# A GEMM by seven products in an fp32 trunk: two of its block sums grow in other buffers, one of them from on-chip memory, and are issued at other steps

## The chip, the cores and the metric

One NeuronCore of a Trainium2 chip runs the whole program. The metric is the device time of one execution in microseconds. "Before" was run three times: 1407.56, 1402.65 and 1401.54 us, median 1402.65.

## The reference

Two layers in float32 on x of 512 x 1024, each a token mixer and a dense MLP, pre-normed and modulated by a conditioning vector. Layer 0 mixes by chunked attention, layer 1 by spatial gating, which is where the change works:

```python
def chunked_spatial_gating(h, w_in, v_gain, w_s, b_s, w_out):
    B, S, _ = h.shape
    nw = S // SG_WINDOW
    z = jax.nn.gelu(h @ w_in, approximate=False)          # 512x1024 @ 1024x6144
    u, v = jnp.split(z, 2, axis=-1)
    v = rms_norm(v, v_gain).reshape(B, nw, SG_WINDOW, SG_GROUPS, SG_HALF // SG_GROUPS)
    ...
    vm = jnp.einsum('gij,bnjgc->bnigc', w, v) + b_s.T.astype(v.dtype)[None, None, :, :, None]
    return (u * vm.reshape(B, S, SG_HALF)) @ w_out
...
def reference(...):
    ...
        x = x + g1 * y
        h = rms_norm(x, norm_ffn[i]) * (1.0 + sc2) + sh2
        x = x + g2 * squared_relu_mlp(h, ffn_w1[i], ffn_w2[i])
```

## The kernel before

**Arithmetic.** Every large product is done in three matmuls (`mm3`, its matmuls are line 92): `Split` makes of a float32 tile its high part, by a cast on ACT (line 485, 128x1024), and the rest, by a subtract on DVE (line 486), and high x high, high x low and low x high are summed.

**Seven products.** `seven` (line 613) multiplies by a 1024x1024 piece of a weight in 2x2 blocks of 512x512, with seven products where the plain way has eight. Each block comes in two halves `s_` = 0, 1 of 512 KB. The names of the right blocks in the code are x = B00, z = B10, w = B01, y = B11. The steps run in the order m = 0, 1, 2, 4, 3, 5, 6; m = 0, 1 and 4 multiply by a block itself (x, z, y), the others by a sum: m = 2 by x after x += w, m = 3 by that x after x += y, m = 5 by B01 + B11, m = 6 by B10 plus the x of m = 3. `own` says which of the four sums DVE makes (`plus`, line 630, from a loaded block). The others are made by a DMA that adds to what is there: `grow`, line 627, issued by GpSimd (POOL), reads 512 KB from DRAM and adds it into a block's buffer.

**Who calls it.** The gate's halves of `b_w_in` (`Gate(p)`, p = 1, 2) had own = (2, 3, 5, 6), all on DVE. `Mix(p)`, p = 0, 1, 2, the other half, had own = (2, 3): its m = 5 and m = 6 sums grow by DMA, twelve DMAs in all (3 passes x 2 sums x 2 halves). The FFN's second product had own = (). A step has four parts, `load`, `right` (sums and Splits), `left` and `mult`, and `Run(steps, 4, 3)` calls a step's load 4 and 3 ticks, and its right and left 3 ticks, ahead of its mult.

**Buffers.** A tile takes one of 49 slots of 4 KB per partition (`Slots`), handed out in the order in which they were freed. So whoever first writes a new tile waits for the last users of the tile that had the slot before; which tile that is follows from the order of all frees.

**Mixing.** When a tile of the gate half is ready, `v_store` (line 1423) stores it to the DRAM tensor `vd` (512 KB, issued by ACT). `row_scales` (line 1547 on) makes the rows' scales from the sums of squares, once the gate is done. `Mix.put` gathers a product's outputs, applies Gelu (line 1585), and `Mix.mix` then scales v (line 1593), splits it (cast on ACT, line 1597, and subtract on DVE, line 1598), mixes the positions by matmuls, multiplies (line 1611), transposes on PE (line 1618) and copies out (line 1622). The program goes gate p = 1, 2, then Mix p = 0, a down projection, Mix p = 1, Mix p = 2, and the second down projection.

**Order of the work.** The engines' orders are made by a scheduler from the program as it is written; in a tile name as `s3_856_7615` the first number is the slot and the second counts the tiles. `tc.issue_after` holds an instruction back, in that order, behind another one.

Of the kernel before, what the change touches and what calls it, by code (L numbers as in the profile page):

```python
# [13 lines left out]
ALU = mybir.AluOpType  # L14
AX = mybir.AxisListType

P = 128
# [8 lines left out]
SGH = 3072  # L26
# [26 lines left out]
def trunk_kernel(  # L53
# [20 lines left out]
    V, A, G, T, SP = nc.vector, nc.scalar, nc.gpsimd, nc.tensor, nc.sync  # L74
# [13 lines left out]
    def bank():  # L88
        return PS.get([P, 512], F32)
# [4 lines left out]
    def mm3(ps, lh, ll, rh, rl, start, stop, more=False):  # L94

        mm(ps, lh, rh, start, False, more)
        mm(ps, lh, rl, False, False, more)
        mm(ps, ll, rh, False, stop, more)
# [278 lines left out]
    loaded = [None]  # L377
# [232 lines left out]

    waited = [None]

    def seven(left, src, y, own=()):


        raw, op, ps = {}, {}, {}

        def block(i, j, s_):
            r0 = i * 512 + s_ * 256
            return src[r0:r0 + 256, j * 512:j * 512 + 512].rearrange("(k p) n -> p k n", p=P)  # L620

        def load(name, i, j, s_):
            raw[name, s_] = t, n = SL.get([P, 2, 512], F32)
            SP.dma_start(t, block(i, j, s_))

        def grow(i, j, name, s_):
            G.dma_start(raw[name, s_][0], block(i, j, s_), accum_op=ALU.add)  # L627

        def plus(a, b, s_):
            V.tensor_tensor(raw[a, s_][0], raw[a, s_][0], raw[b, s_][0], ALU.add)  # L630

        def drop(name, s_):
            SL.free(raw.pop((name, s_))[1])

        def right(m, name, add, s_):

            if m == 2 and 2 in own:
                plus("x", "w", s_)
                if 5 not in own:
                    drop("w", s_)  # L640
            if m == 5 and 5 in own:
                name = "w"
                plus("w", "y", s_)
                drop("y", s_)
            if m == 6 and 6 in own:
                plus("x", "z", s_)
                drop("z", s_)
            loaded = m in (3, 5, 6) and m not in own
            with tc.issue_after(waited[0].ins) if loaded and waited[0] is not None else nullcontext():
                op[m, s_] = Split(raw[name, s_][0], [P, 2, 512])  # L650
            if m == 4 and 3 in own:
                plus("x", "y", s_)
            if add is None:
                if not (m == 1 and 6 in own):
                    drop(name, s_)
            elif {0: 2, 2: 3, 4: 5, 3: 6}[m] not in own:
                grow(*add, name, s_)

        def mult(m, acc, first, outs, done, s_):
            a, b = left.op[m], op.pop((m, s_))  # L660
            for u in range(2):
                if first and s_ == 0:
                    ps[acc, u] = bank()
                p, pi = ps[acc, u]
                c = slice(u * P, u * P + P)
                for k in range(2):
                    kk = 2 * s_ + k
                    ah, al, bh, bl = a.hi[:, kk, c], a.lo[:, kk, c], b.hi[:, k, :], b.lo[:, k, :]
                    mm3(p, ah, al, bh, bl, first and kk == 0, kk == 3, not first)
                if s_:  # L670
                    for i, j, o, whole in outs:
                        y.put(2 * i + u, j, p, o, whole)
                    if done:
                        PS.free(pi)
            b.free()
            if s_:
                left.done(m)

        def prep(m, s_):
            if s_ == 0:  # L680
                left.prep(m)

        add, sub = ALU.add, ALU.subtract
        plan = (
            (0, ("x", 0, 0), ("x", (0, 1)), ("z", True, ((0, 0, add, False),), False)),
            (1, ("z", 1, 0), ("z", None), ("y", True, ((0, 0, add, False),), True)),
            (2, None, ("x", (1, 1)), ("v", True, ((1, 1, add, False),), False)),
            (4, ("y", 1, 1), ("y", (0, 1)), ("v", False, ((0, 1, add, False),), True)),
            (3, None, ("x", (1, 0)), ("z", False, ((0, 1, sub, False),), False)),
            (5, None, ("y", None), ("z", False, ((1, 1, sub, False),), False)),  # L690
            (6, None, ("x", None), ("z", False, ((1, 0, add, True),), True)),
        )

        def loads(m, b, s_):
            if m == 2 and 2 in own:
                load("w", 0, 1, s_)
            if b:
                load(*b, s_)

        return [  # L700
            Step(
                lambda m=m, b=b, s_=s_: loads(m, b, s_),
                lambda m=m, r=r, s_=s_: right(m, *r, s_),
                lambda m=m, s_=s_: prep(m, s_),
                lambda m=m, p=p, s_=s_: mult(m, *p, s_),
            )
            for m, b, r, p in plan for s_ in range(2)
        ]
# [38 lines left out]
    def ffn(l, norm, rows, cols, after, bgn, lag=1):  # L747
# [53 lines left out]
        def down_steps(q):  # L801
            steps = seven(Spent(lambda: quarters(q)), ffn_w2[l][q * 1024:(q + 1) * 1024, :], y)

            def mult_last(f=steps[-1].mult):
                f()
                bg(bgn.pop(0) if bgn else 0)

            steps[-1].mult = mult_last
            return steps
# [606 lines left out]
    kept = Kept(lambda: norm.blocks)  # L1416
# [57 lines left out]
    def gate_steps(cb):  # L1474

        raw, op, ps = {}, {}, {}

        def load(n):
            t, i = raw[n] = SL.get([P, 2, 512], F32)
            c0 = SGH + cb * 512  # L1480
            SP.dma_start(t, b_w_in[0][n * 256:n * 256 + 256, c0:c0 + 512].rearrange("(k p) n -> p k n", p=P))

        def right(n):
            t, i = raw.pop(n)
            op[n] = Split(t, [P, 2, 512])
            SL.free(i)

        def mult(n):
            w = op.pop(n)
            for t in range(NT):  # L1490
                if n == 0:
                    ps[t] = bank()
                a = kept.op[((0, 1), ("r", 6))[t // 2][n // 2]]
                c = slice(t % 2 * P, t % 2 * P + P)
                for k in range(2):
                    kk = n % 2 * 2 + k
                    mm3(
                        ps[t][0], a.hi[:, kk, c], a.lo[:, kk, c], w.hi[:, k, :], w.lo[:, k, :],
                        n == 0 and k == 0, n == 3 and k == 1,
                    )  # L1500
                if n == 3:
                    if t % 2 == 0:
                        vv[cb, t // 2] = SL.get([P, 2, 512], F32)
                    gate_end(cb, t, ps[t][0])
                    PS.free(ps[t][1])
            w.free()
            bg(2 if n == 3 else 1)

        return [
            Step(lambda n=n: load(n), lambda n=n: right(n), nothing, lambda n=n: mult(n)) for n in range(4)  # L1510
        ]
# [3 lines left out]

    steps = gate_steps(1)
    for p in (1, 2):
        steps += seven(kept, b_w_in[0][:, SGH + p * 1024:SGH + (p + 1) * 1024], Gate(p), (2, 3, 5, 6))

    wsT = []  # L1520
    bsT = cp.tile([P, SGG], F32, name="bsT")
# [107 lines left out]
    def then(f, *gs):  # L1629
        def both():  # L1630
            f()
            for g in gs:
                g()

        return both

    y = Sum()
# [8 lines left out]

    def mix_steps(p):
        m = Mix(p)
        out = seven(kept, b_w_in[0][:, p * 1024:(p + 1) * 1024], m, (2, 3))
        out[0].right = then(out[0].right, m.gain, lambda: m.take(0, 0))  # L1650
        for i, hf, b in ((6, 1, 0), (8, 1, 1), (10, 0, 1)):
            out[i].right = then(out[i].right, lambda hf=hf, b=b: m.take(hf, b))
        return out
# [57 lines left out]
    def take(p, j):  # L1711
        return lambda: take_parts(*[(p, i, j) for i in range(2)])

    u, d = [mix_steps(p) for p in range(3)], [down_steps(p) for p in range(2)]
    tail = [Step(nothing, down_ahead, nothing, nothing)]
    for x in u[0] + u[1] + u[2] + d[0] + d[1]:
# [96 lines left out]
```

## Time and profile before

| | |
|---|---|
| runs | 1407.56, 1402.65, 1401.54 us; median 1402.65 |
| profiled execution | 1408.5 us, span 1406.6 us |
| mean granted clock of TensorE | 0.988 of full speed |
| busy share of the span | PE 98%, PE weight loads 84%, DVE 70%, ACT 53%, POOL 6% |
| DMA | 246.68 MB, 175 GB/s in the mean |
| Split, one tile | cast on ACT 1.05 us, subtract on DVE 1.22 us |
| sums of line 630 on DVE | 28, of 1.22 us |
| accumulating DMAs of line 627 from `b_w_in` | 12, of 512 KB |

The profile is of one execution. PE stands for TensorE's matmuls, PEld for its weight loads, DVE for VectorE, ACT for ScalarE, POOL for GpSimd, SP for the engine whose queue issues most loads. Lines are those of the kernel. A row of a timeline gives start and duration and, in brackets, how long the engine was idle before it and what ended that. The clock is the share of 2.4 GHz that TensorE was granted; .50 is 1.2 GHz.

### The profile page before, as it was taken

The page shows a single profiled execution, that of the slowest core. Times are in us where ns is not written, and L with a number is a line of the kernel's source. Part 1 is how long each engine was busy: PE and PEld are TensorE (multiplying, and loading weights), DVE is VectorE, ACT ScalarE, POOL GpSimd, SP SyncE. Part 2 cuts the span into 40 slices and gives each one's busy share as a digit, 9 for nine tenths or more (in the row PEclk, how much of TensorE's full clock was granted, in tenths as well). Part 3 has the DMA queues.
Part 4 walks back from the last instruction along what each step waited for, and adds up shares of the span by engine and source line. Part 5 has one row for each costly group of instructions (what it writes and reads, how often), then busy time and mean ns, then how long its engine had stood idle before and what let it go on. Part 6 is the DMA issues. An engine that isn't in the chain of part 4 may idle for free.

```text
span 1406.6 us, 18894 instructions
## 1 busy us (share of the span) xinstructions
PE 1375.4 (98%) x7130; PEld 1175.7 (84%) x7130; DVE 986.5 (70%) x1430; ACT 744.0 (53%) x1248; POOL 85.4 (6%) x98
## 2 busy tenths in 40 slices
PE   8999999899999999999999899998999999999998
PEld 7899988789888888888888788887889988888887
DVE  5888998775656777677796776677956355665772
ACT  6537667655454545537576554556435454554530
POOL 0000000001101102000000100010000010100100
PEclk8999999999999999999999999999999999999999
DMA  9746576564667776458446657665548276655541
GB/s 373 235 134 211 161 200 186 196 240 120 157 182 185 181 224 122 144 183 302 133 165 204 170 162 216 176 171 182 151 125 268 64 163 180 135 164 128 112 150 60
DMA packets 98251, 246.68 MB, mean 175 GB/s; under 512 B 8680, under 2 KB 10096, under 8 KB 98160
## 3 DMA queue, kind: packets, MB, share of 16 engines
q1 hardware_dynamic: 79536, 205.62, 44.3%
q0 software_dynamic: 16896, 33.56, 14.5%
q10 hardware_dynamic: 1728, 6.29, 1.2%
q8 instruction: 56, 0.92, 0.3%
q14 instruction: 35, 0.29, 0.1%
HBM read 222.37 MB, written 14.68 MB: 169 GB/s over the span
## 4 chain that ended last, share of the span: by engine, by line
PE 78%; issue 9%; DVE 6%; DMA 4%; ACT 2%; SPq 1%; POOL 0%; DVEq 0%; POOLq 0%; ACTq 0%
PE p L92 76%; DMA s<-xsg 1%; DVE s L974 1%; DMA s<-in_a_w_in 1%; DMA vd<-s 1%; DVE s L1213 1%; DVE s L486 0%; SPq L1176 0%; PE p L1251 0%; DMA s<-in_ada_w 0%; PE p L1618 0%; ACT s L485 0%; DMA s<-in_ffn_w 0%; PE p L315 0%; DMA s<-in_x 0%
## 5 line engine op out<-in xcount | busy, mean ns | idle before, releaser
L92 PE MATMUL p<-s,s 128*128 128x512 f32 (+2 forms) x6496 | 1312.4, 362 | 18.5 <-ACT s L485 4.3
L92 PEld LDWEIGHTS p<-s,s 128*128 128x128 f32 x6496 | 1101.2, 190 | 204.0 <-ACT s L485 4.7
L486 DVE TENSOR_TENSOR s<-s,s 128x1024 fp32r<-128x1024 f32 x308 | 370.8, 1221 | 230.7 <-ACT s L485 177.7
L485 ACT CAST s<-s 128x1024 fp32r<-128x1024 f32 x308 | 317.4, 1051 | 206.0 <-PE p L92 110.6
L762 ACT ACTIVATE r<-p 128x512 f32<-128x512 f32 x64 | 38.3, 598 | 126.2 <-PE p L92 126.2
L194 DVE SCALAR_TENSOR_TENSOR s<-s,cs,s 128x1024 f32<-128x1024 f32 x70 | 89.6, 1280 | 12.6 <-DMA s<-in_ada_w 12.0
L627 POOL DMA_DIRECT2D s<-in_ffn_w x48 | 58.3, 1215 | 498.9 <-DVE s L486 395.6
L523 DVE TENSOR_TENSOR s<-s,p 128x512 f32<-128x512 f32 x76 | 50.2, 682 | 15.5 <-PE p L92 15.2
L388 ACT CAST s<-s 128x1024 fp32r<-128x1024 f32 x36 | 37.6, 1051 | 43.0 <-DMA s<-in_ffn_w 13.8
L389 DVE TENSOR_TENSOR s<-s,s 128x1024 fp32r<-128x1024 f32 x36 | 43.4, 1222 | 10.6 <-ACT s L388 10.4
L424 DVE TENSOR_TENSOR tr<-p,s 128x512 f32<-128x512 f32 (+1 forms) x33 | 22.0, 671 | 33.9 <-PE p L92 33.7
L768 ACT ACTIVATE s<-r 128x256 f32<-128x256 f32 (+1 forms) x112 | 44.9, 442 | 1.4
L536 DVE TENSOR_TENSOR s<-s,s 128x1024 f32<-128x1024 f32 x28 | 33.6, 1220 | 10.9 <-PE p L92 10.5
L1218 ACT ACTIVATE s<-s,nm 128x128 f32<-128x128 f32 (+3 forms) x64 | 36.0, 564 | 7.7 <-DVE nm L1213 6.3
L630 DVE TENSOR_TENSOR s<-s,s 128x1024 f32<-128x1024 f32 x28 | 33.9, 1218 | 6.2 <-DMA s<-in_b_w_in 6.1
L319 ACT ACTIVATE tt<-p,mod,mod 128x128 f32<-128x128 f32 x64 | 24.0, 464 | 21.0 <-PE p L315 10.4
L304 ACT ACTIVATE s<-s 128x512 f32<-128x512 f32 x24 | 15.4, 640 | 35.3 <-DVE s L425 34.2
L425 DVE TENSOR_TENSOR s<-s,tr 128x512 f32<-128x512 f32 (+1 forms) x33 | 22.1, 673 | 15.2 <-DMA s<-xsg 14.5
L1256 DVE TENSOR_TENSOR s<-p,s 128x512 fp32r<-128x512 f32 (+3 forms) x64 | 29.2, 482 | 3.9 <-ACT s L1255 3.5
L1213 DVE CUSTOM_DVE_ANT_0 s<-p,s 128x128 f32<-128x128 f32 (+3 forms) x64 | 29.5, 483 | 1.4 <-PE p L92 1.3
L627 POOL DMA_DIRECT2D s<-in_b_w_in x12 | 14.5, 1205 | 236.4 <-DVE s L486 231.9
L1255 ACT CAST s<-p 128x512 fp32r<-128x512 f32 (+3 forms) x64 | 25.2, 427 | 6.3 <-PE p L1251 5.1
(146 smaller groups left out, 770.9 us busy)
## 6 DMA issues: line engine op xcount, KB each, us to landing
s<-in_ffn_w SPq DMA_DIRECT2D x116, 512.0 KB, 4.3
s<-in_ada_w SPq DMA_DIRECT2D x96, 512.0 KB, 5.1
s<-in_ffn_w POOLq DMA_DIRECT2D x48, 512.0 KB, 5.8
s<-in_b_w_in SPq DMA_DIRECT2D x48, 512.0 KB, 4.4
s<-in_b_w_out SPq DMA_DIRECT2D x24, 512.0 KB, 4.7
s<-in_a_w_in SPq DMA_DIRECT2D x22, 512.0 KB, 4.9
s<-s SPq DMA_DIRECT2D x64, 128.0 KB, 3.9
vd<-s ACTq DMA_DIRECT2D x12, 512.0 KB, 3.8
```

Source lines behind the costliest of these rows:

```text
L92: T.matmul(ps, lhsT, rhs, start=start, stop=stop, skip_group_check=more)
L194: V.scalar_tensor_tensor(acc, r, ck, acc, ALU.mult, ALU.add)
L388: A.copy(hi, raw)
L389: engs[len(ids) // 2 % len(engs)].tensor_tensor(lo, raw, f32(hi), ALU.subtract)
L485: A.copy(self.hi, raw)
L486: mark[0] = V.tensor_tensor(self.lo, raw, f32(self.hi), ALU.subtract)
L523: V.tensor_tensor(dst, dst, ps, op)
L627: G.dma_start(raw[name, s_][0], block(i, j, s_), accum_op=ALU.add)
L762: A.activation(r, ps, AF.Relu)
L768: A.activation(d, v, AF.Square)
L1213: V.tensor_tensor_reduce(out=pt[it], in0=ps[:, 0:n], in1=b["bias"][:, 512 - n:512], scale=-1.0, scalar=-NEG, op0=ALU.add, op1=ALU.min, acc ...
L1218: A.activation(pt[it], pt[it], AF.Exp, bias=nm[:, it:it + 1], scale=-1.0, accum_out=sm[:, it:it + 1])
```

## The change

In `Mix` the two sums that are made by DMA move. The m = 5 sum grew in y, y += B01, issued behind the Split of step 4; it now grows in w, w += B11 from DRAM, issued behind step 2's `plus(x, w)` and Split. The m = 6 sum grew in x, x += B10 from DRAM, issued behind the Split of step 3; it now grows in z by a DMA from SBUF to SBUF, z += x, issued behind step 4's `plus(x, y)`. y is given up at step 4 and x at step 3, while z lives on to step 6 and w to step 5. In `Gate` the m = 6 sum is z += x instead of x += z, on DVE. `issue_after` is left at m = 5 and 6 alone. For the FFN own is now None, its code path as before.

```diff
--- before.py
+++ after.py
@@ -610,7 +610,7 @@
 
     waited = [None]
 
-    def seven(left, src, y, own=()):
+    def seven(left, src, y, own=None):
 
 
         raw, op, ps = {}, {}, {}
@@ -634,27 +634,32 @@
 
         def right(m, name, add, s_):
 
-            if m == 2 and 2 in own:
+            if own is None:
+                op[m, s_] = Split(raw[name, s_][0], [P, 2, 512])
+                if add is None:
+                    drop(name, s_)
+                else:
+                    grow(*add, name, s_)
+                return
+            name = {0: "x", 1: "z", 2: "x", 4: "y", 3: "x", 5: "w", 6: "z"}[m]
+            if m == 2:
                 plus("x", "w", s_)
+            elif m in own:
+                plus(*{5: ("w", "y"), 6: ("z", "x")}[m], s_)
+                drop({5: "y", 6: "x"}[m], s_)
+            late = m in (5, 6) and m not in own and waited[0] is not None
+            with tc.issue_after(waited[0].ins) if late else nullcontext():
+                op[m, s_] = Split(raw[name, s_][0], [P, 2, 512])
+            if m == 2 and 5 not in own:
+                grow(1, 1, "w", s_)
+            elif m == 4:
+                plus("x", "y", s_)
                 if 5 not in own:
-                    drop("w", s_)
-            if m == 5 and 5 in own:
-                name = "w"
-                plus("w", "y", s_)
-                drop("y", s_)
-            if m == 6 and 6 in own:
-                plus("x", "z", s_)
-                drop("z", s_)
-            loaded = m in (3, 5, 6) and m not in own
-            with tc.issue_after(waited[0].ins) if loaded and waited[0] is not None else nullcontext():
-                op[m, s_] = Split(raw[name, s_][0], [P, 2, 512])
-            if m == 4 and 3 in own:
-                plus("x", "y", s_)
-            if add is None:
-                if not (m == 1 and 6 in own):
-                    drop(name, s_)
-            elif {0: 2, 2: 3, 4: 5, 3: 6}[m] not in own:
-                grow(*add, name, s_)
+                    drop("y", s_)
+                if 6 not in own:
+                    G.dma_start(raw["z", s_][0], raw["x", s_][0], accum_op=ALU.add)
+            elif m in (5, 6) or m == 3 and 6 not in own:
+                drop(name, s_)
 
         def mult(m, acc, first, outs, done, s_):
             a, b = left.op[m], op.pop((m, s_))
@@ -692,7 +697,7 @@
         )
 
         def loads(m, b, s_):
-            if m == 2 and 2 in own:
+            if m == 2 and own is not None:
                 load("w", 0, 1, s_)
             if b:
                 load(*b, s_)
@@ -1515,7 +1520,7 @@
 
     steps = gate_steps(1)
     for p in (1, 2):
-        steps += seven(kept, b_w_in[0][:, SGH + p * 1024:SGH + (p + 1) * 1024], Gate(p), (2, 3, 5, 6))
+        steps += seven(kept, b_w_in[0][:, SGH + p * 1024:SGH + (p + 1) * 1024], Gate(p), (5, 6))
 
     wsT = []
     bsT = cp.tile([P, SGG], F32, name="bsT")
@@ -1646,7 +1651,7 @@
 
     def mix_steps(p):
         m = Mix(p)
-        out = seven(kept, b_w_in[0][:, p * 1024:(p + 1) * 1024], m, (2, 3))
+        out = seven(kept, b_w_in[0][:, p * 1024:(p + 1) * 1024], m, ())
         out[0].right = then(out[0].right, m.gain, lambda: m.take(0, 0))
         for i, hf, b in ((6, 1, 0), (8, 1, 1), (10, 0, 1)):
             out[i].right = then(out[i].right, lambda hf=hf, b=b: m.take(hf, b))
```

The order that the scheduler made, at three places. The first is POOL, all accumulating DMAs of Mix, passes p = 0, 1, 2 in turn (L660 is the DMA from on-chip memory). Before:

```order
L627 DMA s8_839_7467<-in_b_w_in 128x2x512
L627 DMA s19_843_7512<-in_b_w_in 128x2x512
L627 DMA s27_822_7352<-in_b_w_in 128x2x512
L627 DMA s13_818_7330<-in_b_w_in 128x2x512
L627 DMA s26_941_8229<-in_b_w_in 128x2x512
L627 DMA s17_945_8282<-in_b_w_in 128x2x512
L627 DMA s6_905_8002<-in_b_w_in 128x2x512
L627 DMA s11_915_8047<-in_b_w_in 128x2x512
L627 DMA s27_995_8672<-in_b_w_in 128x2x512
L627 DMA s0_999_8693<-in_b_w_in 128x2x512
L627 DMA s21_967_8465<-in_b_w_in 128x2x512
L627 DMA s20_972_8488<-in_b_w_in 128x2x512
```

and now:

```order
L627 DMA s36_831_7418<-in_b_w_in 128x2x512
L627 DMA s48_836_7449<-in_b_w_in 128x2x512
L660 DMA s5_825_7371<-s13_818_7330 128x1024
L660 DMA s6_828_7399<-s27_822_7352 128x1024
L627 DMA s47_932_8161<-in_b_w_in 128x2x512
L627 DMA s10_937_8196<-in_b_w_in 128x2x512
L660 DMA s4_928_8124<-s37_915_8047 128x1024
L660 DMA s5_920_8083<-s30_905_8002 128x1024
L627 DMA s5_984_8587<-in_b_w_in 128x2x512
L627 DMA s26_989_8613<-in_b_w_in 128x2x512
L660 DMA s37_975_8506<-s17_967_8465 128x1024
L660 DMA s47_978_8528<-s30_972_8488 128x1024
```

Each pass had two DMAs into y and two into x; it now has two into w and two into z, the latter reading x. All lines behind the diff's place have numbers that are higher by five in the changed kernel.

The second is where the gate's last tile is stored and Mix's first products begin. On ACT before (L1423 is the store, s3_856 the high part of x for m = 3):

```order
L1450 ACTIVATE s3_842_7479<-p7_318_7197 128x512
L485 CAST s37_860_7637<-s27_822_7352 128x1024
L1452 ACTIVATE vq_7481,vss_3669<-s3_842_7479 128x512
L1450 ACTIVATE s3_842_7479<-p3_319_7204 128x512
L1452 ACTIVATE vq_7490,vss_3669<-s3_842_7479 128x512
L1423 DMA vd_3668<-s3_842_7479 128x1024
L1585 ACTIVATE s42_848_7543<-s42_848_7543 128x512 x2
L485 CAST s3_856_7615<-s13_818_7330 128x1024
```

and now on ACT (L1428 is the store, s38_856 the high part of x for m = 3):

```order
L1455 ACTIVATE s17_842_7479<-p7_318_7197 128x512
L1457 ACTIVATE vq_7481,vss_3669<-s17_842_7479 128x512
L1455 ACTIVATE s17_842_7479<-p3_319_7204 128x512
L485 CAST s38_856_7617<-s13_818_7330 128x1024
L1586 COPY s42_848_7544<-p2_325_7525 128x512
L485 CAST s0_860_7638<-s27_822_7352 128x1024
L1457 ACTIVATE vq_7490,vss_3669<-s17_842_7479 128x512
L1428 DMA vd_3668<-s17_842_7479 128x1024
L1590 ACTIVATE s42_848_7544<-s42_848_7544 128x512 x2
L1586 COPY s30_859_7629<-p0_328_7603 128x512
```

and on DVE now (s17_855 is the low part of y for m = 4, the second half; L1554 to L1555 are the row scales):

```order
L486 TENSOR_TENSOR s11_857_7618<-s13_818_7330,s38_856_7617 128x1024
L1589 TENSOR_TENSOR s42_848_7544<-s42_848_7544,p5_326_7559 128x512
L486 TENSOR_TENSOR s31_861_7639<-s27_822_7352,s0_860_7638 128x1024
L1589 TENSOR_TENSOR s42_848_7544<-s42_848_7544,p6_327_7566 128x512
L1554 TENSOR_REDUCE vs4_7493<-vss_3669 128x4
L486 TENSOR_TENSOR s17_855_7598<-s19_843_7512,s10_854_7597 128x1024
L145 TENSOR_SCALAR ra_7495<-vs4_7493 128x4
L146 TENSOR_SCALAR ry_7496<-ra_7495 128x4
```

Before, the cast that follows the store's issue on ACT writes the slot that the store reads, s3. Now the stored tile is in s17, and the next tile in that slot is written by DVE's subtract, which stands between the reduction and the rest of the row scales.

The third is the end of the last pass, on ACT. Before (s18_1033 is the high part of x for m = 6, L1597 the cast of a scaled v):

```order
L1597 CAST s32_1040_9021<-vh_9019 128x512
L1581 COPY s9_1028_8931<-p2_383_8830 128x512
L485 CAST s37_1030_8942<-s0_999_8693 128x1024
L485 CAST s18_1033_8960<-s21_967_8465 128x1024
L1597 CAST s6_1038_9000<-vh_8998 128x512
L485 CAST s19_1044_9061<-s42_982_8565 128x1024
L485 CAST s0_1042_9041<-s44_1024_8917 128x1024
L485 CAST s36_1046_9065<-s47_993_8650 128x1024
```

and now (s16_1033 is the high part of z for m = 6, L1602 the cast of a scaled v):

```order
L1586 COPY s19_1028_8931<-p4_382_8825 128x512
L1602 CAST s32_1040_9021<-vh_9019 128x512
L1586 COPY s19_1028_8931<-p2_383_8832 128x512
L485 CAST s27_1030_8942<-s26_989_8613 128x1024
L485 CAST s16_1033_8960<-s37_975_8506 128x1024
L1602 CAST s24_1038_9000<-vh_8998 128x512
L485 CAST s36_1046_9065<-s6_993_8650 128x1024
L485 CAST s22_1049_9071<-s17_1029_8940 128x1024
```

The Split for m = 6 stands ahead of the same cast in both, and reads the buffer into which the last pass's accumulating DMA writes: s21_967 before, s37_975 now.

## Rows read from the trace of the kernel before

**Rows 1.** The page of the profiled execution: the row of its part 1 (busy us, share of the span and instructions of each engine) and one of its part 5, the groups of instructions (line, engine, operation, tiles, shapes, count | busy us, mean ns of one | idle time before them and what ended most of it).

```profile
PE 1375.4 (98%) x7130; PEld 1175.7 (84%) x7130; DVE 986.5 (70%) x1430; ACT 744.0 (53%) x1248; POOL 85.4 (6%) x98
...
L486 DVE TENSOR_TENSOR s<-s,s 128x1024 fp32r<-128x1024 f32 x308 | 370.8, 1221 | 230.7 <-ACT s L485 177.7
```

**Rows 2.** Waits of PE between 690 and 1060 us: what PE waited for, us in total, times, longest. These are all its waits in that stretch.

```profile
PE p L92 <- ACT s L485: 4.3, 1, 4.3
PE p L92 <- ACT s L1597: 3.3, 1, 3.3
PE p L92 <- DVE s L1584: 1.0, 1, 1.0
```

**Rows 3.** Timeline of PE, 760 to 1060 us: start, us, line, operation, tiles, count, and in brackets the idle time before the row and what ended it.

```profile
790.72 14.97 PE L92 MATMUL p<-s,s 128*128 128x512 f32 x59 [4.31 <-ACT s L485]
...
942.49 6.57 PE L92 MATMUL p<-s,s 128*128 128x512 f32 x30
952.32 0.33 PE L92 MATMUL p<-s,s 128*128 128x128 f32 x1 [3.27 <-ACT s L1597]
```

**Rows 4.** Timeline of ACT, 776 to 797 us, the same columns (ACTq is ACT's queue: issues of DMAs).

```profile
780.29 0.33 ACTq L1423 DMA_DIRECT2D vd<-s  x1
...
789.62 1.04 ACT L485 CAST s<-s 128x1024 fp32r<-128x1024 f32 x1 [7.26 <-DMA vd<-s]
```

**Rows 5.** The chain of waits, 775 to 800 us, in order of time: start, us, what.

```profile
780.29 9.25 DMA vd<-s
```

**Rows 6.** The DMA stores of line 1423 (tensor vd), all of the program: issue to landing.

```profile
DMA to landing us min/median/max: 2.6/3.8/9.2
```

**Rows 7.** Timeline of POOL, 755 to 945 us: the accumulating DMAs of Mix (the row's time is POOL's own part of the issue).

```profile
778.64 1.21 POOL L627 DMA_DIRECT2D s<-in_b_w_in  x1 [5.14 <-DVE s L486]
780.71 1.20 POOL L627 DMA_DIRECT2D s<-in_b_w_in  x1 [0.86 <-DVE s L486]
...
934.23 2.44 POOL L627 DMA_DIRECT2D s<-in_b_w_in  x2 [49.99 <-DVE s L486]
937.05 1.20 POOL L627 DMA_DIRECT2D s<-in_b_w_in  x1 [0.38 <-DVE s L486]
```

**Rows 8.** Timeline of ACT, 938 to 958 us.

```profile
950.71 1.04 ACT L485 CAST s<-s 128x1024 fp32r<-128x1024 f32 x1 [4.16 <-DMA s<-in_b_w_in]
951.66 0.61 ACT L1597 CAST s<-vh 128x512 fp32r<-128x512 f32 x1
```

**Rows 9.** DMA issues between 930 and 955 us: tiles, queue, count, KB each, median us to landing.

```profile
s<-in_b_w_in POOLq DMA_DIRECT2D x4, 512.0 KB, 11.8
```

**Rows 10.** The accumulating DMAs of line 627, all of the program: POOL's own part of an issue in ns (min/median/max), and issue to landing.

```profile
L627 POOL DMA_DIRECT2D s<-in_b_w_in x12: 1203/1203/1218, 772.3 to 939.2; - x12
...
DMA to landing us min/median/max: 5.7/6.1/15.5
```

**Rows 11.** Busy time by stretch around 786 us: us, then busy us (and instructions) of PE, PEld, DVE, ACT, POOL, then the granted clock, the share of the 16 DMA engines, GB/s.

```profile
786.00:790.80 4.80, 0.49 (x3) 0.08 (x1) 0.14 (x2) 1.18 (x2) 0.00 (x0) 0.79 1.07 291
790.80:792.00 1.20, 1.20 (x3) 1.01 (x4) 1.20 (x2) 1.20 (x3) 0.00 (x0) 0.50 0.50 184
792.00:794.00 2.00, 2.00 (x6) 1.54 (x6) 1.39 (x2) 2.00 (x4) 1.20 (x1) 0.50 0.08 30
794.00:796.00 2.00, 2.00 (x7) 1.59 (x6) 2.00 (x4) 0.57 (x1) 0.00 (x0) 0.61 0.91 90
```

**Rows 12.** Busy time by stretch around 950 us, columns as in the stretches above.

```profile
949.00:953.70 4.70, 0.42 (x3) 0.23 (x2) 1.92 (x3) 2.99 (x4) 0.00 (x0) 0.88 1.05 296
953.70:955.00 1.30, 1.30 (x3) 1.11 (x4) 1.30 (x2) 1.30 (x2) 0.00 (x0) 0.50 0.12 41
955.00:957.00 2.00, 2.00 (x6) 1.52 (x6) 2.00 (x4) 2.00 (x4) 0.00 (x0) 0.50 0.02 8
957.00:959.00 2.00, 2.00 (x7) 1.52 (x6) 1.88 (x3) 2.00 (x4) 0.00 (x0) 0.50 0.01 4
959.00:961.00 2.00, 2.00 (x11) 1.83 (x10) 1.81 (x3) 2.00 (x4) 0.00 (x0) 0.90 0.00 0
961.00:965.00 4.00, 4.00 (x24) 3.34 (x23) 4.00 (x8) 2.71 (x5) 0.00 (x0) 1.00 0.23 61
```

**Rows 13.** Timeline of DVE, 905 to 940 us: the sums of line 630 in the last pass.

```profile
907.17 1.22 DVE L630 TENSOR_TENSOR s<-s,s 128x1024 f32<-128x1024 f32 x1
...
913.35 1.22 DVE L630 TENSOR_TENSOR s<-s,s 128x1024 f32<-128x1024 f32 x1
...
931.34 1.22 DVE L630 TENSOR_TENSOR s<-s,s 128x1024 f32<-128x1024 f32 x1
...
933.61 1.22 DVE L630 TENSOR_TENSOR s<-s,s 128x1024 f32<-128x1024 f32 x1
```

**Rows 14.** The page's part 6, DMA issues: the copies from on-chip memory to on-chip memory (count, KB each, median us to landing).

```profile
s<-s SPq DMA_DIRECT2D x64, 128.0 KB, 3.9
```

**Rows 15.** Timelines of SP (issues of the loads of the last pass) and, the last row, of ACT (the first Split of that pass's x), 865 to 925 us.

```profile
880.34 0.38 SPq L624 DMA_DIRECT2D s<-in_b_w_in  x1
...
887.53 17.36 SPq L624 DMA_DIRECT2D s<-in_b_w_in  x4
...
899.58 1.05 ACT L485 CAST s<-s 128x1024 fp32r<-128x1024 f32 x1
```

## The prediction

> **What bounds the kernel now.** I read the engines' shares first: PE is busy for 1375.4 us of 1406.6, 98%, and the next engine, DVE, for 70% [rows 1]. So PE's matmuls are the floor; the change leaves their work as it is, and it can only give or take what PE idles and what a lowered clock costs. 31 us of idle time are left in all. The change works in the second layer's gate and mix, so I then read PE's waits there: between 690 and 1060 us there are three, 4.3, 3.3 and 1.0 us, 8.6 in sum [rows 2]. The timeline puts them at two places: A, before the row at 790.72, and B, before the one at 952.32 (the 3.3 us, with the 1.0 right behind it) [rows 2, 3]. Everything else in that stretch is matmul after matmul, and no transfer, cast or sum there is worth anything unless it stands behind A or B.
>
> *Place A, who is late.* PE waits for a Split's cast on ACT (line 485). That cast started at 789.62, after 7.26 us in which ACT waited for a store to vd [rows 4]. The store was issued at 780.29 and took 9.25 us [rows 4, 5], against 3.8 in the median of the twelve [rows 6]. The order of before says why a cast waits for a store: its output is s3_856, and slot 3 held s3_842, the gate tile which this last store reads. Beside it went the accumulates that POOL issued at 778.64 and 780.71 [rows 7].
>
> *Place B, who is late.* PE waits for the cast at 951.66 (line 1597), which stands in ACT's queue behind a Split's cast at 950.71; this one waited 4.16 us for an accumulating DMA from in_b_w_in [rows 8]. It is the Split of x for m=6 in the last pass. Its accumulate is the one POOL issued at 937.05, third of four within 5 us [rows 7]; it took 950.7 - 937.05, some 13.6 us, where the median of all is 6.1 and of these four 11.8 [rows 9, 10].
>
> *What follows each wait.* The granted clock falls to .50, the level of 1.2 GHz, behind both: PE does 6 matmuls in 2 us there, and 24 in 4 us when the clock is back at 1.00 [rows 11, 12]. Behind A the loss is 1.2 x .50 + 2 x .50 + 2 x .39 = 2.4 us [rows 11]; behind B 1.3 x .50 + 2 x .50 + 2 x .50 + 2 x .10 = 2.9 us [rows 12]. So A costs 4.3 + 2.4 = 6.7 us, and B 4.3 + 2.9 = 7.2 us: 13.9 together.
>
> **The change, part by part.** *Gate, p = 1, 2.* The m=6 sum is now z += x where it was x += z, both by DVE at 1.22 us; the same count of instructions. PE's order is the same up to 700 us. Cost 0: PE waits nowhere between 690 us and A [rows 2, 3], so the matmuls hide it.
>
> *Mix, the m=5 sum.* It was y += B01 from DRAM, issued behind step 4's Split of y; now it is w += B11, issued behind the sum x += w of step 2. Six accumulates stay six, 512 KB each; the issue costs POOL 1.2 us, and POOL is 6% busy. In the last pass they follow the sums that stood at 907.17 and 913.35 [rows 13], instead of being issued at 934.23; they have some 25 us more. Cost 0, hidden by three steps of matmuls.
>
> *Mix, the m=6 sum.* It was x += B10 from DRAM, issued behind step 3's Split; now it is z += x, on chip, issued behind x += y of step 4, whose sums stood at 931.34 and 933.61 [rows 13]. The first can go at about 932.6 + 0.5, some 4 us before 937.05, and two accumulates are in flight where there were four. Reads from DRAM fall by six times 512 KB.
>
> *The price of an on-chip accumulate* stands in no row. Below it lies the copy on chip of 128 KB, 3.9 us [rows 14]; above it the slowest accumulate from DRAM, 15.5, with 5.7 and 6.1 as minimum and median [rows 10]. I take 6.1: size, queue and operation are those of the row, and only the source differs. The Trainium skill ("DMA: Bandwidth & Descriptors", section "Anatomy of one DMA — SWDGE (gpsimd) path") fits GpSimd's transfers as 2.0 us plus the bytes at 436 GB/s; by that 512 KB would be an estimated 3.2 us, and B would go as well. No accumulate here is that quick: the fastest took 5.7 us [rows 10].
>
> *Place B after.* The Split of z for m=6 now waits for an accumulate issued at some 933. PE ran dry at 949.05 (952.32 - 3.27, [rows 3]), and cast and cast take 1.04 + 0.61 [rows 8], so it must land by 947.4: 14.4 us are there, against 6.1 taken. Even at the 13.6 us of before it fits. B goes: -7.2.
>
> *Place A after.* In the changed order the cast for m=3 writes slot 38, which no store holds. The store's slot (17 now) is given to the low half of step 4's second Split, which DVE writes ahead of the row scales (lines 1554, 145 to 152, 1555). So the wait for the store does not vanish, it moves to DVE. PE has 29 matmuls more in front of it there, 29 x 0.219 = 6.4 us (0.219 is 6.57 / 30, [rows 3]), so that PE asks for that half at about 786.4 + 6.4 = 792.8. The store goes out at about 782.5 by my count (a cast and a copy more stand ahead of it), and one accumulate goes beside it instead of two. At the median 3.8 it lands at 786.3. Behind the low half (1.22, [rows 1]) DVE has some 6 us of row scales, gains and subtracts before the first mixing matmul, which PE reaches at about 795.2; so a landing of up to 5.6 us costs nothing, and 9.25 costs 3.7. I take 1 us, nearer to the median. A: -6.7 + 1 = -5.7.
>
> *Longer lives of tiles.* w and z stay in their slots for more steps, 49 slots being handed on in the order in which they were freed. In the last pass SP's loads of x's second half and of z now stand behind the previous pass's on-chip accumulates (their slots are the x tiles which these read). They were issued at 880.34 and 887.53, and the first cast of that x started at 899.58 [rows 15]. An accumulate issued at about 876 and taking 6.1 lands at 882, before most of these loads; counting matmuls in front at 0.219 us I get some 19 us until PE would feel it. Cost 0. Behind SP's waiting load its queue holds only loads that are needed later.
>
> *Sum:* -7.2 - 5.7 = -12.9, so the profiled execution of 1408.5 becomes 1395.6. That execution is 5.85 above the median of the runs, 1402.65; against the median it would be 1389.8. Some of the 5.85 is probably in A and B themselves (their transfers vary from 2.6 to 9.2 and from 5.7 to 15.5), and this part can't be gained twice. I forecast between the two: 1392.
>
> **The rivals.**
>
> *One place stays* (A's wait comes back at DVE). For it: the store took 9.25 us beside accumulates, and one is still beside it; against it: it is one, where there were two, and it is issued 3 us ahead of the store. Only B is gained, 7.2: 1401.3 against the profiled run, 1395.5 against the median. Chance 0.22.
>
> *Nothing nets out.* Landing at the last pass depends on something other than the four transfers' crowding: its start is held up while DVE works, as it does behind each sum. For it: these four were issued in a dense stretch of DVE and landed in 11.8 us in the median, against 6.1 [rows 9, 10]; against it: POOL's own part took 1203 to 1218 ns in all twelve issues, with DVE 70% busy [rows 1, 10]. The Trainium skill ("SBUF — State Buffer", section "SBUF: two separate sides") has such a rule: a DMA issued from GpSimd waits for its descriptors while DVE holds the port that both share. By that rule crowding would not be the cause, and fewer transfers would not help. If landing is slow there for such a reason, it stays near 13.6 or passes 14.4, B keeps half its wait and A the store's: about 1402. Chance 0.13.
>
> *Slower: the on-chip accumulate is dear.* It reads and writes the same memory, on the one queue, and three things now hang on it: the Split at m=6 from 14.4 us on, the loads of the next pass from about 19, by the same count the first down projection's loads from about 30. At 25 us a piece PE would wait 10.6 and 6, with a lowered clock of 2.9 behind each [rows 12]: +22.4 - 13.9 = +8.5, 1411. It decides from about 24 us, 1.6 times the slowest accumulate that a row shows [rows 10] and 6 times the copy on chip [rows 14]. Chance 0.08.
>
> That the change does not do what it says is no rival here: the order shows the six on-chip accumulates and the earlier issues where the text has them.
>
> **How the numbers follow.** My forecast has 0.57, at 1392 with its own range 1387 to 1397 (the two reckonings 1389.8 and 1395.6, and 2 either way for the store's landing and the runs' scatter). A measurement of this kernel tells about 0.5%, 7 us, from no change: faster means below 1395.6, slower above 1409.7. Of my forecast 0.50 lie below 1395.6, of the first rival 0.07: faster 0.57. The rest of both, and the second rival: same 0.35. The third: slower 0.08. The range 1386 to 1405 takes in the first two rivals, and leaves out the dear accumulate and some of the tails.
>
> **What would show it.** Right: no wait of PE over 1 us between 900 and 1000 us, a clock of 1.00 there, and the Split for m=6 not ending a wait for a DMA; at 786 us PE's wait gone or under 2 us, and any wait for the vd store on DVE. On-chip accumulates landing in 4 to 8 us. Wrong: the on-chip accumulates at 14 us or more; a wait of DVE's line 486 for vd of over 5 us with PE idle behind it; or new waits of SP's line 624 that PE ends up behind at 880 to 920 us.

## The result and the profile after

The changed kernel takes 1395.72 us in the median (five runs, 1394.16 to 1397.79) against 1402.87 for the kernel before on the same chip: a ratio of 0.9942, 95% interval 0.9929 to 0.9956. The profiled execution took 1395.72 us, where that of before took 1408.5.

PE is still the floor, busy for 98% of a shorter span, and for 7.2 us less than in [rows 1] with the same 7130 matmuls:

```profile
PE 1368.2 (98%) x7130; PEld 1171.2 (84%) x7130; DVE 985.6 (71%) x1430; ACT 742.5 (53%) x1248; POOL 83.4 (6%) x98
```

The waits of PE between 690 and 1060 us, columns as in [rows 2], 8.6 us there:

```profile
PE p L315 <- DVE s L306: 0.8, 1, 0.8
PE p L1623 <- DVE s L1616: 0.6, 1, 0.6
PE p L92 <- DVE s L1589: 0.5, 1, 0.5
```

1.9 us are left. PE's timeline runs through A without a gap, where [rows 3] had 4.31 us, and near B only the 0.63 are left, in front of another instruction:

```profile
693.17 105.55 PE L92 MATMUL p<-s,s 128*128 128x512 f32 x469
...
951.29 0.98 PE L1623 MATMUL p<-ident,s 128*128 128x128 f32 x4 [0.63 <-DVE s L1616]
```

The granted clock stays at 1.00 in both stretches (same columns as [rows 11, 12]):

```profile
786.00:790.80 4.80, 4.80 (x23) 3.97 (x22) 4.32 (x18) 2.61 (x5) 0.00 (x0) 1.00 0.95 332
...
949.00:953.70 4.70, 3.94 (x19) 2.98 (x19) 4.70 (x8) 4.59 (x7) 0.00 (x0) 1.00 0.34 112
953.70:961.00 7.30, 7.30 (x39) 6.23 (x38) 7.30 (x9) 1.11 (x3) 0.00 (x0) 1.00 0.33 91
```

At A, the last store to vd was issued at 780.75. DVE's low half that takes its slot now is the row at 785.24, and has no bracket: the store had landed, if only just (780.75 + 4.4 = 785.15). The store before it did hold DVE for 6.95 us, at 777.34, with PE not noticing:

```profile
777.34 1.23 DVE L486 TENSOR_TENSOR s<-s,s 128x1024 fp32r<-128x1024 f32 x1 [6.95 <-DMA vd<-s]
...
785.24 1.21 DVE L486 TENSOR_TENSOR s<-s,s 128x1024 fp32r<-128x1024 f32 x1
```

The DMA issues from 778 to 784 us (median us to landing; one each) give 4.4 us for that store, against 9.25 in [rows 5]:

```profile
s<-s POOLq DMA_DIRECT2D x1, 512.0 KB, 7.2
vd<-s ACTq DMA_DIRECT2D x1, 512.0 KB, 4.4
```

POOL's accumulates in the first and the last pass (line 660 is the one on chip). They stand apart now, where [rows 7] has two 2 us apart at A and four within 5 us at B:

```profile
761.07 1.21 POOL L627 DMA_DIRECT2D s<-in_b_w_in  x1 [72.40 <-DVE s L1454]
764.31 1.20 POOL L627 DMA_DIRECT2D s<-in_b_w_in  x1 [2.04 <-DVE s L630]
766.74 0.90 POOL L660 DMA_DIRECT2D s<-s  x1 [1.23 <-ACT s L485]
780.38 0.86 POOL L660 DMA_DIRECT2D s<-s  x1 [12.73 <-ACT vq L1457]
...
924.41 0.90 POOL L660 DMA_DIRECT2D s<-s  x1 [15.30 <-DVE s L630]
931.45 0.86 POOL L660 DMA_DIRECT2D s<-s  x1 [6.14 <-DVE s L630]
```

The on-chip accumulates, POOL's part in ns and us to landing (min/median/max), and those from DRAM, landing, both of the whole program:

```profile
L660 POOL DMA_DIRECT2D s<-s x6: 861/881/903, 766.7 to 931.5; - x6
...
DMA to landing us min/median/max: 4.5/5.8/9.5
```

```profile
DMA to landing us min/median/max: 5.6/5.9/10.4
```

The two profiled executions lie 12.8 us apart; 6.7 of it are waits of PE in this stretch (8.6 to 1.9), 5.3 what the lowered clock cost (2.4 and 2.9), and 0.8 lies elsewhere.

### The profile page after: what moved, and what is told of

Read it like the earlier page. It is cut to its first block, busy times and chain, and to the rows that moved or that the text cites. A ratio compares the mean times of both kernels' runs of the same rounds, so it can differ in the third digit from the quotient of the medians.

```text
span 1393.7 us, 18907 instructions
## 1 busy us (share of the span) xinstructions
PE 1368.2 (98%) x7130; PEld 1171.2 (84%) x7130; DVE 985.6 (71%) x1430; ACT 742.5 (53%) x1248; POOL 83.4 (6%) x98
## 4 chain that ended last, share of the span: by engine, by line
PE 86%; DVE 6%; DMA 4%; ACT 2%; issue 1%; SPq 1%; DVEq 0%; ACTq 0%
PE p L92 83%; DMA s<-in_ada_w 1%; DMA s<-in_a_w_in 1%; DMA s<-xsg 1%; PE p L1623 1%; DVE s L979 1%; DMA s<-s 1%; PE p L1256 1%; ACT s L485 1%; SPq L1181 0%; DVE s L425 0%; PE p L315 0%; DMA s<-vd 0%; DVE s L1218 0%; DVE tr L424 0%
## 5 line engine op out<-in xcount | busy, mean ns | idle before, releaser
L1627 ACT COPY s<-p 128x512 f32<-128x512 f32 x24 | 13.8, 583 | 26.2 <-PE p L1623 26.2
```

## The experiments

Six kernels (e2 to e5, e9, e10) come from one version of `right`, in which the change has three switches: GZ, the gate's m = 6 sum in z; MW, Mix's m = 5 sum in w; MZ, Mix's m = 6 sum in z, on chip. With all off its order of instructions is that of before, with all on that of after. Its core for Mix:

```python
            if m == 2:
                plus("x", "w", s_)
                if not gate and not MW:
                    drop("w", s_)
            ...
                op[m, s_] = Split(raw[name, s_][0], [P, 2, 512])
            ...
            if m == 1 and not MZ:
                drop("z", s_)
            elif m == 2 and MW:
                grow(1, 1, "w", s_)
            elif m == 4:
                plus("x", "y", s_)
                if MW:
                    drop("y", s_)
                else:
                    grow(0, 1, "y", s_)
                if MZ:
                    G.dma_start(raw["z", s_][0], raw["x", s_][0], accum_op=ALU.add)
            elif m == 3:
                if MZ:
                    drop("x", s_)
                else:
                    grow(1, 0, "x", s_)
            elif m in (5, 6):
                drop(name, s_)
```

| run | what it is | median us | ratio to before, 95% interval |
|---|---|---|---|
| e1 | before once more | 1405.45 | 1.0007 (0.9994 to 1.0020) |
| e2 | GZ alone | 1403.83 | 0.9994 (0.9983 to 1.0004) |
| e3 | MW alone | 1396.92 | 0.9942 (0.9928 to 0.9957) |
| e4 | MZ alone | 1404.80 | 1.0001 (0.9992 to 1.0010) |
| e5 | MW and the old accumulates into y as well | 1407.00 | 1.0031 (1.0016 to 1.0047) |
| e6 | before, one slot held back | 1400.33 | 0.9976 (0.9964 to 0.9988) |
| e7 | after, z += x on DVE | 1395.82 | 0.9947 (0.9931 to 0.9963) |
| e8 | after, both sums on DVE | 1401.26 | 0.9978 (0.9969 to 0.9987) |
| e9 | MW in the first pass alone | 1402.03 | 0.9978 (0.9966 to 0.9990) |
| e10 | MW in the last pass alone | 1399.67 | 0.9965 (0.9951 to 0.9979) |

Before had 1404.83 in the median beside e1 to e4, 1404.51 beside e5 to e8, 1404.86 beside e9 and e10.

### e1: the kernel before, another execution

> The kernel before, once more, with a profile of another execution. Theory 1 (two stalls: A, the slot whose last reader is the store to vd, at 786 us; B, the Split that waits for the last pass's crowded accumulate, at 949 us; each with a stretch at half the clock behind it): the time moves from execution to execution with these two, since both hang on how a transfer lands; ratio 1.000 within 0.003, PE's waits between 690 and 1060 us between 2 and 9 us, at the same two places. Rival (the 5.9 us by which the profiled execution lay over the median came from elsewhere): 8 to 9 us of waits there again whatever the time of the execution.

This execution took 1405.34 us. PE's waits, and the stretches behind A (790:792) and B (the rest), columns as in [rows 11, 12]:

```profile
PE p L92 <- ACT s L485: 2.8, 1, 2.8
PE p L92 <- ACT s L1597: 2.5, 1, 2.5
PE p L92 <- DVE s L1584: 1.2, 2, 0.9
```

```profile
790.00:792.00 2.00, 1.52 (x6) 1.16 (x7) 1.54 (x2) 2.00 (x5) 0.01 (x1) 1.00 1.06 347
...
951.00:952.00 1.00, 0.99 (x2) 0.83 (x3) 1.00 (x2) 1.00 (x2) 0.00 (x0) 0.50 0.92 352
952.00:954.00 2.00, 2.00 (x6) 1.58 (x5) 2.00 (x3) 2.00 (x4) 0.00 (x0) 0.50 0.04 15
954.00:956.00 2.00, 2.00 (x6) 1.52 (x6) 2.00 (x3) 2.00 (x3) 0.00 (x0) 0.50 0.00 0
956.00:958.00 2.00, 2.00 (x12) 1.73 (x11) 1.72 (x3) 2.00 (x3) 0.00 (x0) 0.92 0.02 4
```

The same two places, with other sizes. A cost 2.8 us, and the clock behind it stayed at 1.00; B cost 2.5 + 0.9 of waits and 0.5 + 1.0 + 1.0 + 0.16 = 2.7 of clock, 6.1 in all. Without the two this execution comes to 1405.34 - 8.9 = 1396.4, that of [rows 3] to 1408.5 - 13.9 = 1394.6, and after took 1395.72. So A and B are the gain to within 2 us, and A is most of what made the first profile a dear one. The size of B hardly moved (7.2 and 6.1).

### e2, e3, e4: the three parts alone

> Only the gate's part of the change (z += x instead of x += z, both on DVE); Mix as before. Theory 1: nothing is gained; the last store's tile changes its slot, but the next tile in that slot is again the high part for m = 3, written by a cast on ACT, so A and B stay: 1403, ratio 0.998 to 1.002. Rival (the gate's other order of frees is what shifts the slots): A gone, 1399.

> Only the m = 5 sum of Mix moves (w += B11, issued at step 2); the m = 6 sum stays x += B10 from DRAM behind step 3's Split, the gate is as before. Theory 1: A stays (the slot of the last store still goes to the cast for m = 3), B goes, since two accumulates instead of four are in flight at 934 us: 1399, ratio 0.996 to 0.999; profile: PE waits for line 485 behind vd<-s at about 786 us, 2 to 4.5 us, and no wait over 1 us at 949 us. Rival (the crowding by accumulates makes the store late, and so A too): 1396, no wait over 1 us at either place.

> Only the m = 6 sum of Mix moves (z += x on chip, issued at step 4); the m = 5 sum stays y += B01 from DRAM, issued at step 4 as well, the gate is as before. Theory 1: A goes, since z lives longer and the slot of the last store now goes to DVE's low part for m = 4; at 934 us four accumulates are in flight again, but the one for m = 6 goes out some 4 us earlier, so B shrinks to 0 to 2 us: 1397 to 1399, ratio 0.995 to 0.998. Rival (the crowding makes B, whatever the issue time): B stays with 3 to 4 us of waits, 1400.

e2 moved nothing, as expected: A (2.3 us) and B were both there. e3 alone gives the whole gain; A is gone as well, as the rival had it, and there theory 1 was wrong. The slot of the last store still goes to the cast for m = 3, which waited 1.68 us for it, and PE never noticed:

```profile
784.17 1.05 ACT L485 CAST s<-s 128x1024 fp32r<-128x1024 f32 x1 [1.68 <-DMA vd<-s]
```

because the store landed in 3.7 us (DMA issues of e3, 778 to 784 us), with one accumulate beside it:

```profile
vd<-s ACTq DMA_DIRECT2D x1, 512.0 KB, 3.7
s<-in_b_w_in POOLq DMA_DIRECT2D x1, 512.0 KB, 7.0
```

At B two accumulates landed in 8.0 us in the median (920 to 960 us), where four took 11.8 [rows 9]:

```profile
s<-in_b_w_in POOLq DMA_DIRECT2D x2, 512.0 KB, 8.0
```

and the longest wait of PE in 690 to 1060 us is:

```profile
PE p L92 <- DVE s L1626: 1.0, 1, 1.0
```

Theory 1 falls for A: not the slot but the company of the store decides. Theory 2, from here on: at both places PE pays for the number of accumulates in flight beside the transfer that it waits for.

e4 moved the slot as I had foreseen, and gained nothing in all (1397 to 1399 expected). Its waits of PE:

```profile
PE p L92 <- ACT s L1625: 6.2, 2, 5.1
PE p L92 <- DVE s L1612: 1.5, 1, 1.5
```

The chain of waits of e4, 776 to 805 us, shows why: the store takes 7.4 us, DVE's low half (787.17) waits for it, the accumulate into y is issued behind that half and lands at 797.0, and the Split for m = 5 (797.02) stands on ACT ahead of the casts that mixing waits for:

```profile
779.73 7.42 DMA vd<-s
...
787.17 1.24 DVE s L486
...
788.92 8.07 DMA s<-in_b_w_in
...
797.02 1.06 ACT s L485
```

Thus the rival for A in the prediction, the wait that comes back at DVE, is what this slot does beside the old accumulates: 5.1 us, and the clock at .50 behind it, which costs 2.1 more. It does so by way of the accumulate into y, which the change moves away; so e4 does not show what the slot would do without it. At B four accumulates are in flight. The earlier issue takes 4.3 us of waits down to 2.6, and the clock stays at 1.00: B costs 2.6 where it was 6.1 to 7.2. What is left begins with a Split that waits for an accumulate from DRAM, one into y, and not for the one on chip:

```profile
947.52 2.00 ACT L485 CAST s<-s 128x1024 fp32r<-128x1024 f32 x2 [1.75 <-DMA s<-in_b_w_in]
```

So e4 gained some 4 us at B and lost about as much at A.

### e5: the old crowding put back

The edit, against e3 (cut):

```diff
             elif m == 4:
                 plus("x", "y", s_)
-                if MW:
-                    drop("y", s_)
-                else:
-                    grow(0, 1, "y", s_)
+                grow(0, 1, "y", s_)
...
             elif m in (5, 6):
                 drop(name, s_)
+                if m == 5:
+                    drop("y", s_)
```

> As e3_w_only (the m = 5 sum in w, early), and the old accumulates y += B01 are issued as well, at their old place behind step 4's Split; nothing reads their result, y is given up at step 5 as before. So 18 accumulates, with the crowding of before at 780 and 934 us, and the Split for m = 5 depends on none of the late ones. Theory 2 (formed on e3 and e4: what makes the store late at A and the accumulate late at B is the number of accumulates in flight beside them): the store to vd lands in 7 to 9 us again instead of 3.7, and the accumulates at 934 us in 11 to 12 instead of 8; A and B are back with 2 to 4.5 us each: 1402 to 1406, ratio 0.998 to 1.001. Rival (the earlier issue of the m = 5 sum itself is the gain, as its Split no longer waits): 1397, ratio 0.994 to 0.996.

The store took 8.0 us again, the four accumulates at 934 us 11.4 in the median:

```profile
vd<-s ACTq DMA_DIRECT2D x1, 512.0 KB, 8.0
```

```profile
s<-in_b_w_in POOLq DMA_DIRECT2D x4, 512.0 KB, 11.4
```

and PE waits at both places again (4.3 us at 789, 2.1 + 0.2 + 0.6 + 0.9 at 956 to 959). ACT's rows at the two:

```profile
787.42 1.04 ACT L485 CAST s<-s 128x1024 fp32r<-128x1024 f32 x1 [6.78 <-DMA s<-in_b_w_in]
...
952.94 1.99 ACT L485 CAST s<-s 128x1024 fp32r<-128x1024 f32 x2 [6.48 <-DMA s<-in_b_w_in]
```

So an early m = 5 sum brings nothing if the crowding stays: theory 2 holds for the landings. For A's wait it is no clean proof. The 787.42 row waits for an accumulate, not the store: by the order of this program it is a later Split, whose output (s19_883) has the slot of a y (s19_843) that is still being written, a wait that before did not have. It is part of why e5 came out above the range expected.

### e6, e9, e10: one place at a time

e6, in the kernel before (cut):

```diff
         A.dma_start(vd[cb, b], v.rearrange("p t n -> p (t n)"))
-        SL.free(i)
+        stores[0] += 1
+        if stores[0] == 12:
+            held.append(i)
+        else:
+            SL.free(i)
...
+        if p == 0:
+            out[8].right = then(out[8].right, lambda: SL.free(*held))
```

e9 and e10, in e3:

```diff
-            GZ, MW, MZ = 0, 1, 0
+            GZ, MW, MZ = 0, not gate and y.p == 0, 0
```

(y.p == 2 in e10).

> The kernel before, in which only the slot of the last stored gate tile is given back later (at Mix's ninth step instead of at once), so that the cast for m = 3 takes another slot; the transfers stay as they are. This is A alone: theory 2 has the store land in 7 to 9 us still, with nobody of weight waiting; PE's wait at 786 us gone, the one at 949 us stays with 3 to 4 us: 1400 to 1402, ratio 0.997 to 0.999 (2.5 to 4 us less). Rival (as in e4 the wait only moves to the mixing matmuls, or to another tile): 1404, ratio 1.000.

> As e3_w_only, but the m = 5 sum moves to w in Mix's first pass alone; the second and last pass as before. Theory 2 (accumulates in flight beside the transfer that PE waits for): at A one accumulate is beside the store instead of two, it lands in 3.5 to 5 us and PE's wait at 786 us goes; at B the four accumulates of before are in flight, 11 to 12 us, and 3 to 4 us of waits stay, with the lower clock behind them: about 1400, as e6 gave by another way, ratio 0.996 to 0.998. Rival (A and B are not two separate places, one removes or feeds the other): 1396 or 1404.

> As e3_w_only, but the m = 5 sum moves to w in Mix's last pass alone. Theory 2: A is as before (two accumulates beside the store, it lands in 7.5 to 9 us, PE waits 2 to 4.5 us at 786 us), at B two accumulates are in flight instead of four, they land in about 8 us, and PE's waits at 949 us stay under 1 us with the clock at 1.00: about 1400, ratio 0.996 to 0.998; with e9's gain it adds up to that of e3 (0.994). Rival: 1404 or 1396, the places not being separate.

e6 takes away who waits at A, e9 what makes the store late; both leave B. PE's waits of e6, then of e9, with e9's store:

```profile
PE p L92 <- ACT s L1602: 2.6, 1, 2.6
PE p L92 <- DVE s L1589: 1.8, 2, 1.0
```

```profile
PE p L92 <- ACT s L1625: 2.7, 1, 2.7
PE p L92 <- DVE s L1612: 1.4, 2, 1.0
...
PE p L92 <- ACT s L485: 0.5, 1, 0.5
```

```profile
vd<-s ACTq DMA_DIRECT2D x1, 512.0 KB, 5.5
```

A is gone in e6 (the other 0.8 us of its DVE row stand at 799 us), though its store still took 7.2. In e9 A is down to 0.5 us, the store at 5.5, above the 3.5 to 5 expected. B has 2.6 and 1.0, 2.7 and 1.0. e10 is the mirror, A with 2.3 us, and B gone, two accumulates at 8.1 us:

```profile
PE p L92 <- ACT s L485: 2.3, 1, 2.3
```

The ratios say the same: e9 takes 0.22%, e10 0.35%, together 0.57%; e3 takes 0.58%, each known to some 0.15% either way. So the two places are separate as far as the runs can tell, and A is worth 3 to 4 us (e9, e6), B 5 (e10), each give or take 2.

### e7, e8: sums on DVE instead

The edit of e7, in the kernel after:

```diff
-        out = seven(kept, b_w_in[0][:, p * 1024:(p + 1) * 1024], m, ())
+        out = seven(kept, b_w_in[0][:, p * 1024:(p + 1) * 1024], m, (6,))
```

and `(5, 6)` in e8.

> The kernel after, with Mix's m = 6 sum (z += x) made by DVE at step 6 instead of by the on-chip DMA; six accumulates are left, six DVE sums of 1.22 us are added. Theory 2: nothing of weight was waiting for that DMA in after, and DVE has room; 1394 to 1397, ratio to before 0.993 to 0.996, waits of PE under 2.5 us in 690 to 1060 us. Rival (DVE, 71% busy, is too tight at 790 and 945 us): a new wait of PE of 2 us or more there, 1398 to 1401.

> The kernel after, with both of Mix's sums made by DVE (own = (5, 6), as in the gate): no accumulating DMA between 690 and 1060 us, twelve DVE sums of 1.22 us more. Theory 2: the stores to vd land in 4 us, no transfer is late, and what is left is DVE's own load: 1394 to 1398, ratio 0.993 to 0.997. Rival (DVE becomes late at the Splits for m = 5 and 6): waits of PE of 2 to 5 us behind line 486 or the mixing's subtract, 1399 to 1403.

e7 is after's equal; the longest wait of PE in it:

```profile
PE p L92 <- DVE s L1603: 1.0, 1, 1.0
```

The on-chip DMA is therefore not needed for the gain, nor does it harm. The last store to vd, with no accumulate beside it, landed in 2.9 us (DMA issues of e7, 778 to 784 us):

```profile
vd<-s ACTq DMA_DIRECT2D x1, 512.0 KB, 2.9
```

e8 took the rival's time, but not at the places that the rival names. PE's waits in 690 to 1060 us are 5.0 us where after has 1.9, and behind those at 798 to 801 us the clock fell to .50, 1.7 us more: together most of the 5.5 us between the two profiles. Its longest wait stands behind DVE's multiply of the mixing (as do 0.9 us more; 0.7 stand behind line 486),

```profile
PE p L1623 <- DVE s L1616: 1.5, 1, 1.5
```

and the store to vd took 6.8 us with no accumulate in flight at all. What DMAs were issued between 774 and 790 us:

```profile
s<-vd SPq DMA_DIRECT2D x2, 512.0 KB, 4.7
s<-in_b_w_out SPq DMA_DIRECT2D x2, 512.0 KB, 3.8
vd<-s ACTq DMA_DIRECT2D x1, 512.0 KB, 6.8
```

So a store can be late without an accumulate beside it, where theory 2 had 4 us. What made this one late is not shown: when it was issued, at 780.18, one of the reads of vd was under way, as in e3, where the store took 3.7. Whether e8 lost to the twelve DVE sums or to DVE's wait for this store (2.8 us) was not separated.

## Why the prediction was right, and where it was not

- **The number.** 1395.72 lies in the range, 3.7 us above the 1392. By itself it could not tell the forecast from the first rival, which had 1395.5 against the median for a kernel in which only B goes; the profile does, since A's wait is gone. The median also misses the mark for faster, 1395.6, by 0.1 us, though the interval of the ratio leaves 1 out.
- **The bound and the two places.** Right. Outside PE's waits from 690 to 1060 us and the clock behind A and B the two profiles differ by 0.8 us, and the loss at A and B is the gain (e1's sum, e9 and e10).
- **B.** Right in cause and size: crowding of four accumulates, 7.2 us forecast, 6.1 in e1's execution, about 5 in e10's runs. In e3 two accumulates issued at the old time land in 8 us. The forecast gave this to the earlier issue and to the fewer transfers together; e3 shows that fewer are enough, e4 that earlier issue alone takes B down to 2.6 us but does not remove it.
- **A.** Right that it goes, wrong in the reason. The step that failed is "the cast for m = 3 writes slot 38, which no store holds", with the wait moved to DVE under cover. That slot gained nothing beside the old accumulates (e4: a landing of 7.4 us cost 5.1 of wait, where the text had 3.7 for 9.25), and with the old slot A goes as well (e3). A slot that nobody needs soon did remove A under the old crowding (e6). What I had put second, one accumulate beside the store instead of two, is the cause: 3.7 to 5.5 us with one in flight (e3, after, e9) against 7.2 to 9.25 with two or three (before, e1, e2, e4, e5, e6, e10). In after it went out 0.4 us ahead of the store, not 3. With none the store took 2.9 (e7), but also 6.8 (e8), so their number is not all that counts. The plain loads beside it were not the same in all of these; in e3 and e5 they were alike up to the store (three reads of vd, issued from 772.7 and from 770.9 us), and there the accumulates alone make 8.0 of 3.7, in one profile of each. Of the 1 us kept for the store, nothing was paid in after.
- **The size of A.** 6.7 us were taken from one execution; in e1 A cost 2.8, in e2 and e10 2.3, since the wait was shorter and the clock did not fall behind it. This is the mis-sized term: profile against profile the sum was 12.9 and came to 12.8, run against run it is 7.2 by the medians beside after's (and 8.7 by those beside e7's, its equal). That 12.8 is so near is partly luck: A gave all its 6.7 and not 5.7, and the 1.9 us of waits that after has stood in no sum. The text put a part of the 5.85 us between profile and median to A and B. The two cost 5.0 us more in it than in e1's execution, so it was nearly all, and by that estimate 1392 should have been 1395 or 1396.
- **The on-chip accumulate.** Forecast at 6.1 us, measured 5.8 in the median, 4.5 to 9.5, where 4 to 8 was to be the sign. The Trainium skill's fit ("DMA: Bandwidth & Descriptors", section "Anatomy of one DMA — SWDGE (gpsimd) path"), an estimated 3.2 us, is below all six; the measurement decides. The longest landing on chip, 9.5, is far from the 24 us that the slower rival needed.
- **The rival of a held-up start.** Against it: the four late accumulates became quicker when two of them were moved away, with DVE no less busy around them (for 12.0 of the 15 us from 930 on in e3 and e10, for 10.95 in before). That GpSimd's descriptors wait while DVE holds the port that both share, as the Trainium skill has it ("SBUF — State Buffer", section "SBUF: two separate sides"), no row here shows: POOL's part of an issue stayed at 1203 ns or so from DRAM, 861 to 903 on chip.
- **The gate, the longer lives of tiles, SP's loads.** Cost 0 as forecast (e2, and no wait over 0.8 us in after from 690 to 1060 us).

## What to carry to other kernels

When the bounding engine waits for a transfer, look first at which other transfers are in flight beside it, and move those that have slack; here issuing two of four accumulates early was the whole gain (e3), and making the other sum on chip added none (e7). Giving the waiter another buffer helps if nothing behind the new waiter leads back to the same engine: one held slot did it (e6), a slot passed to DVE did not (e4). Take a second profile before sizing a stall that hangs on a landing time: the same stall cost 6.7, 2.8 and 2.3 us.

## What was not expected of the hardware

- The last 512 KB store to vd landed in 2.9 us (e7) to 9.25 us (before). With one accumulate in flight it took 3.7 to 5.5, with two or three 7.2 or more; the 6.8 of e8, with none, stay unexplained.
- An accumulate from on-chip memory was no quicker to land than one from DRAM: 5.8 against 5.9 us in the median of after. Only POOL's part is shorter, 881 against some 1203 ns.
- A wait of 2.8 us at A left the granted clock at 1.00, one of 2.5 at B in the same execution lowered it to .50 (e1; it is .74 in the mean of 949 to 950 us, and PE's first matmul after that wait started at 949.67, so the 0.9 us that followed came too late to be the reason). What PE did before the two was matmul after matmul in both; why they differ stays open.
